# Ten pairs of gate and up blocks by seven products instead of nine, with the squares' sum and the gating moved into the first two pairs

## The chip, the core and the metric

The kernel runs on one core of a Trainium2 chip. A core has five engines with a queue each, worked off in order: TensorE (PE in the profile, its weight loads PEld), VectorE (DVE), ScalarE (ACT), GpSimd (POOL) and SyncE (SP), which here only issues DMAs. The metric is the device time of one execution in microseconds. The change is compared with the kernel before on the same chip.

## The reference

Two layers of an encoder trunk for 512 tokens of width 1024, all in float32: an attention, then a gated feed-forward block (2816 wide), both with a normalisation before and after. What the change touches is the feed-forward part and the last products of the attention ahead of it:

```python
def rms_norm(x, g):
    y = xf * lax.rsqrt(jnp.mean(xf * xf, axis=-1, keepdims=True) + EPS)
    return (y * g.astype(jnp.float32)).astype(x.dtype)

def swiglu(h, w_gate, w_up, w_down):
    return (jax.nn.silu(h @ w_gate) * (h @ w_up)) @ w_down

for layer in range(DEPTH):
    h = rms_norm(x, attn_pre_g[layer])
    ...
    x = x + rms_norm(y, attn_post_g[layer])
    h = rms_norm(x, ffn_pre_g[layer])
    f = swiglu(h, ffn_w_gate[layer], ffn_w_up[layer], ffn_w_down[layer])
    x = x + rms_norm(f, ffn_post_g[layer])
```

## The kernel before

**Tiles.** Activations lie feature by feature: a tile is [128 features, 512 tokens], x is eight of them. Every matmul operand is split into a high part (a cast to the fast float32 form, on ACT) and a low part (the difference, on DVE), and each product takes three matmuls: high by high, high by low, low by high (`mm3`, L375; `split`, L143). Weights come in pieces of [128, 1024]: `Feed` holds the order of all pieces (`plan`), loads them through a ring of five raw tiles on SP's queue and splits them one or two pieces ahead of their use, into rings of three high and three low tiles, or, where a piece is planned with room "h", into tiles of the feed-forward pool.

**Order.** The program is traced in Python, and a planner then puts each engine's queue in order: the instruction that is traced first goes first, if its operands and its tile are there in the planner's own reckoning. `first(n)` lets instructions count as traced n earlier, and `issue_after` (`behind`) sets one instruction behind another on the same queue, without a wait. A tile is taken from a ring with a tag when its first instruction is placed, and is free again when its last one is done. Tag "u" has 39 tiles of [128, 512] (L78, L87), tag "h" 40 (L1136). PSUM has eight banks: four with tag "mm", two with "s", two with "t" (L93).

**Stages of a layer.** Attention; `out_proj` (L683), whose last four output tiles are made in two token halves; `Post.add_half` (L631), which sums the squares of a half (`Sum.total`: transposes on TensorE into a bank "t", a sum on DVE), takes the power -1/2 on POOL (`rstd`, L478) and spreads the factor with transposes (`spread`, L494); `apply`, which adds the normalised result to x and splits the new x (xs, 16 tiles "u"). Then gate and up. Of 22 blocks of 128 features, 0 and 1 are done in token halves (L1147), so that TensorE can begin when half of x is there; 2 and 3 whole (L1184); the other 18 as nine pairs in `products` (L1514). The norm's factor (from the squares of x, L161 and L164, total and spread at L1173 to 1178) is not in xs; it multiplies the gate's output (L1193, L1561).

**A pair by seven products.** Two blocks of gate and the same of up, by two halves of the tokens (A0, A1) and two halves of the features, are a 2 by 2 block product; seven products of half-size operands replace eight. The token side's combinations (tb, 16 tiles "u") are built once a layer by `blocks_of` in three steps; the weight side's are made for each pair: a pair's pieces are loaded twice for two sums, the sums begun by DMAs that add (`Pair.begin`, on POOL's queue, behind the plain load) and continued by two DVE additions (`Pair.sums`, L183). For the first pair of a layer DVE makes the first two sums as well. A pair's products go to the banks `be` (products 0 and 6; two banks, "s" in even pairs, "t" in odd ones), `al` (1, 3, 4, 5) and `ga` (2). Results are copied or added out of the banks after each product into two gate and two up tiles (tag "u"). After product 6 the pair is gated: times the factor (DVE), Silu (ACT), times up (DVE, into `hd`), and for every second block four differences that the down projection needs (`Hidden.add`, L1251). The down projection (`down`) works by seven products too. In layer 1, steps of `by_tokens` (loads of x, DVE transposes, stores) are put between the pairs' products.

Of the kernel before, what the change touches and what calls it, by code (L numbers as in the profile page):

```python
# [19 lines left out]
KT = D // P  # L20
# [7 lines left out]
N_WHOLE = 4  # L28
# [40 lines left out]
def trunk(ctx: ExitStack, tc: tile.TileContext, a, out):  # L69
# [80 lines left out]

    class Pair:
# [4 lines left out]
        def __init__(self, src):  # L156
            self.src, self.raw, self.then, self.made = src, {}, None, False

        def tile(self, n, pool_=wp, tag="raw", bufs=5):
            t = pool_.tile([P, 1024], F32, tag=tag, name=name_("raw"), bufs=bufs)  # L160
            nc.sync.dma_start(t, self.src[n])  # L161
            return t

        def begin(self):  # L164

            r, self.made = self.raw, True
            r[0] = r[3] = r[6] = self.tile(2, wide[0], "sum", 2)
            r[4] = self.tile(2, wide[0], "sum2", 2)
            for j, n in ((0, 3), (4, 0)):
                nc.gpsimd.dma_start(r[j], self.src[n], accum_op=OP.add)  # L170

        def load(self, j):

            if j == 0:
                if not self.made:
                    self.raw[4] = self.tile(2, wide[0], "sum2", 2)
                self.raw[5] = self.tile(3)
            elif j in (1, 2):
                self.raw[j] = self.tile(j - 1)

        def sums(self, j):
# [81 lines left out]
    class Feed:  # L263


        def __init__(self):
            self.plan, self.raw, self.ready, self.pos, self.room = [], [], [], 0, {}
            self.behind, self.gate = {}, None
# [4 lines left out]
        def add_pairs(self, src):  # L273
# [3 lines left out]
            for p, pair in enumerate(pairs):  # L277
                pair.then = pairs[p + 1] if p + 1 < n else None
                for j in range(7):
# [8 lines left out]
        def load(self, i):  # L288
            while len(self.raw) <= min(i, len(self.plan) - 1):
# [5 lines left out]
                if isinstance(src, Pair):  # L295
                    src.load(j)
# [8 lines left out]
        def split(self, i):  # L305
            while len(self.ready) <= min(i, len(self.plan) - 1):
# [32 lines left out]
                for c in range(0, 0 if isinstance(raw, list) else n, w):  # L339
                    m = min(w, n - c)  # L340
                    with ExitStack() as st:
                        for b in self.behind.get(j, ()):
                            st.enter_context(tc.issue_after(b.ins))
                        if gain is None or isinstance(src, Pair):
                            split(pieces[c // w][0][:, :m], pieces[c // w][1][:, :m], raw[:, c:c + m])
                            continue
                        for d in range(0, m, S):
                            split_scaled(pieces[c // w][0][:, d:d + S], pieces[c // w][1][:, d:d + S],
                                         raw[:, c + d:c + d + S], gain[:, (c + d) // S, 0:1])
# [127 lines left out]

    def rstd(v):  # L478
        r = small("r")[:, :v.shape[1]]
        nc.gpsimd.tensor_tensor(r, v, mhalf[:, :v.shape[1]], op=OP.pow)  # L480
# [128 lines left out]
    class Post:  # L609
# [21 lines left out]
        def add_half(self, h, banks, rest, n1, n2, end=None):  # L631
# [3 lines left out]
            if end:  # L635
                feed.behind[feed.pos] = feed.behind[feed.pos + 1] = ins
# [4 lines left out]
            with first(200):  # L641
                r = rstd(v)
            at = some(rest, n2)
# [31 lines left out]
    def fetch(src, make=U):  # L675
        x = []
        for k in range(KT):
            t = make(name="x")
            nc.sync.dma_start(t, src[:, k])
            x.append(t)  # L680
        return x

    def out_proj(rhs, n_k, post, have, n_last, late):  # L683
# [35 lines left out]
        for h in range(2):  # L719
            k = KT - sum(last)  # L720
            for i, m in enumerate(last):
# [14 lines left out]
                k += m  # L736
        return b
# [110 lines left out]
    for k in range(KT):  # L848
# [17 lines left out]
        if k == 3:  # L866
# [261 lines left out]
    def ffn(i, x_src, osp, firsts, late=()):  # L1128
# [10 lines left out]
        x = fetch(x_src)  # L1139
        post = Post(G_APOST[i], H)  # L1140
        last = out_proj(osp, KT, post, firsts, 2, late)
# [25 lines left out]
        tb = []  # L1167
        more = blocks_of(x, G_FPRE[i], H, tb)
        next(more)
        b = [bank(), bank()]  # L1170
        rest = proj(2, KT, 4, xs, b)
        some(rest, 3)
        v = sx.sum.total()  # L1173
        r = rstd(v)
        eps = sp.tile([P, 4], F32, tag="eps", name=f"eps_{i}", bufs=1)
        V.tensor_scalar(eps, v, EPS, None, op0=OP.mult)
        some(rest, 7)
        rb = spread_sb(r)
        next(more)
        banks.extend(b)  # L1180
        hid = Hidden(H)


        for f in range(N_WHOLE):  # L1184
            if f < 3:
# [666 lines left out]
```

## Time and profile before

| | us |
|---|---|
| median of 3 runs | 1108.43 (1107.37 to 1109.54) |
| the profiled execution | 1108.42 |
| its span, first to last instruction | 1106.5 |
| layer 0: gate and up, blocks 2 and 3 | 213.3 to 236.0 |
| layer 0: nine pairs | 236.0 to 415.7 |
| layer 1: blocks 2 and 3 | 790.1 to 812.9 |
| layer 1: nine pairs | 812.9 to 993.1 |

Times in the views are microseconds from the span's start. A row of the timeline is start, length, engine, line, operation, output <- inputs, count, and in brackets how long the engine had been idle and what ended that. A row of groups is line, engine, operation, shapes, count, then busy time, mean length in ns, idle time before. A matmul is shown with a modelled end that overlaps the next one, so the pace of matmuls is read from a stretch and its count, not from a row's length. L145 is the low part and L144 the high part, whatever is split.

### The profile page before, as it was taken

To read this page: it belongs to the slowest core of one execution; us is meant where nothing else is said; L and a number is where in the kernel's file an instruction comes from. 1 tells how busy PE (TensorE), PEld (TensorE's weight loads), DVE (VectorE), ACT (ScalarE), POOL (GpSimd) and SP (SyncE) were. 2 spreads that over 40 slices of the span, in tenths; PEclk is the share of its full clock that TensorE was granted. 3 is DMA by queue.
4 is the path that set the end of the run, shared out by engine and by line. 5 is a ranking of instruction groups with operands and counts; after the bars stand their busy time and mean duration, and the time that the engine had idled before them with its cause. 6 is when DMAs were issued, how large, how long until landed. Compare 5 with 4: busy or idle time off the path is not lost. (4 is left out here: it accounts for less than half of the span.)

```text
span 1106.5 us, 19053 instructions
## 1 busy us (share of the span) xinstructions
PE 1092.9 (99%) x6893; PEld 978.6 (88%) x6893; DVE 908.8 (82%) x1651; ACT 679.0 (61%) x1319; POOL 118.2 (11%) x181
## 2 busy tenths in 40 slices
PE   9999999999999999999999999999999999999997
PEld 6887889999999998888888888889999999998885
DVE  7787747988878879978867888758988888889977
ACT  7575736755555556668635767656745555556675
POOL 2211100001000001500000110001000010002301
PEclk9999999999999999999999999999999999999999
DMA  7344227427677757961556677636438778859913
GB/s 239 117 118 138 66 69 256 153 76 193 171 205 182 178 171 247 160 193 47 190 146 169 166 193 189 162 115 215 162 92 214 207 198 220 210 177 280 172 29 76
DMA packets 88334, 181.47 MB, mean 164 GB/s; under 512 B 26816, under 2 KB 28608, under 8 KB 88240
## 3 DMA queue, kind: packets, MB, share of 16 engines
q1 hardware_dynamic: 74752, 147.10, 42.8%
q0 software_dynamic: 13056, 32.73, 16.7%
q8 instruction: 54, 0.88, 0.3%
q10 hardware_dynamic: 432, 0.44, 0.1%
q14 instruction: 40, 0.33, 0.1%
HBM read 148.88 MB, written 10.88 MB: 144 GB/s over the span
## 5 line engine op out<-in xcount | busy, mean ns | idle before, releaser
L144 ACT CAST whi<-raw 128x1024 fp32r<-128x1024 f32 (+3 forms) x224 | 225.4, 1006 | 218.2 <-PE al L1544 71.3
L145 DVE TENSOR_TENSOR wlo<-raw,whi 128x1024 fp32r<-128x1024 f32 (+3 forms) x224 | 261.0, 1165 | 62.9 <-ACT whi L144 61.9
L1544 PE MATMUL al<-th,whi 128*128 128x256 f32 x432 | 123.0, 285 | 0.2 <-ACT gt L1554 0.2
L1544 PE MATMUL al<-tl,whi 128*128 128x256 f32 x432 | 121.0, 280 | 0.0
L1544 PE MATMUL al<-th,wlo 128*128 128x256 f32 x432 | 121.0, 280 | 0.0
L376 PE MATMUL b<-xh,whi 128*128 128x512 f32 (+1 forms) x298 | 115.1, 386 | 0.0
L377 PE MATMUL b<-xl,whi 128*128 128x512 f32 (+1 forms) x298 | 109.9, 369 | 0.0
L378 PE MATMUL b<-xh,wlo 128*128 128x512 f32 (+1 forms) x298 | 109.5, 368 | 0.3 <-DVE wlo L145 0.3
L1544 PEld LDWEIGHTS al<-th,whi 128*128 128x128 f32 x432 | 81.3, 188 | 2.6 <-ACT gt L1554 0.4
L1544 PEld LDWEIGHTS al<-tl,whi 128*128 128x128 f32 x432 | 81.3, 188 | 0.0
L1544 PEld LDWEIGHTS al<-th,wlo 128*128 128x128 f32 x432 | 81.3, 188 | 0.0
L545 ACT ACTIVATE p<-p,mn 128x128 f32<-128x128 f32 (+1 forms) x96 | 54.1, 563 | 39.2 <-DVE mn L543 37.4
L145 DVE TENSOR_TENSOR ptl<-pt,pth 128x128 fp32r<-128x128 f32 (+1 forms) x96 | 46.6, 486 | 32.9 <-ACT pth L144 31.3
L145 DVE TENSOR_TENSOR wlo<-wd,whi 128x512 fp32r<-128x512 f32 x86 | 56.3, 685 | 14.6 <-ACT whi L144 14.4
L170 POOL DMA_DIRECT2D raw<-in_w_pair x32 | 28.0, 876 | 367.8 <-DMA raw<-in_w_pair 148.5
L378 PEld LDWEIGHTS b<-xh,wlo 128*128 128x128 f32 x298 | 56.2, 189 | 10.2 <-DVE wlo L145 0.7
L144 ACT CAST whi<-wd 128x512 fp32r<-128x512 f32 x86 | 49.8, 619 | 24.5 <-PE al L1300 10.7
L376 PEld LDWEIGHTS b<-xh,whi 128*128 128x128 f32 x298 | 56.5, 190 | 5.7 <-ACT whi L144 0.2
L377 PEld LDWEIGHTS b<-xl,whi 128*128 128x128 f32 x298 | 56.5, 190 | 5.5
L144 ACT CAST pth<-pt 128x128 fp32r<-128x128 f32 (+1 forms) x96 | 40.3, 422 | 30.3 <-PE pt L558 29.4
L1300 PE MATMUL al<-whi,pl 128*128 128x512 f32 x132 | 51.5, 390 | 0.0
L1300 PE MATMUL al<-whi,ph 128*128 128x512 f32 x132 | 51.4, 389 | 0.0
(319 smaller groups left out, 3301.0 us busy)
## 6 DMA issues: line engine op xcount, KB each, us to landing
raw<-in_w_pair SPq DMA_DIRECT2D x88, 512.0 KB, 4.4
raw<-in_w_pair POOLq DMA_DIRECT2D x32, 512.0 KB, 8.0
wd<-in_w_down SPq DMA_DIRECT2D x54, 256.0 KB, 6.0
raw<-in_w_o SPq DMA_DIRECT2D x16, 512.0 KB, 3.5
raw<-in_w_gu SPq DMA_DIRECT2D x16, 512.0 KB, 4.9
raw<-in_w_down SPq DMA_DIRECT2D x16, 512.0 KB, 4.2
raw<-in_w_qkb SPq DMA_DIRECT2D x16, 512.0 KB, 3.5
wd<-in_w_down POOLq DMA_DIRECT2D x22, 256.0 KB, 5.2
```

Source lines behind the costliest of these rows:

```text
L144: return (nc.scalar.copy(dst_hi, src), V.tensor_tensor(dst_lo, src, dst_hi.bitcast(F32), op=OP.subtract))
L145: V.tensor_tensor(dst_lo, src, dst_hi.bitcast(F32), op=OP.subtract))
L170: nc.gpsimd.dma_start(r[j], self.src[n], accum_op=OP.add)
L376: nc.tensor.matmul(o, l[0], r[0], start=start, stop=False)
L377: nc.tensor.matmul(o, l[0], r[1], start=False, stop=False)
L378: last_mm[0] = nc.tensor.matmul(o, l[1], r[0], start=False, stop=stop)
L545: nc.scalar.activation(p[:, :n], p[:, :n], AF.Exp, bias=mn[:, :1], scale=-1.0, accum_out=self.sums[:, qt:qt + 1])
L1300: nc.tensor.matmul(to[e], l[c], r[d], start=j < 4 and k == 0 and n == 0, stop=k == NF // 2 - 1 and n == 2, skip_group_check=True)
L1544: nc.tensor.matmul(o, l[c], r[d], start=first_ and n == 0, stop=k == K2 - 1 and n == 2, skip_group_check=True)
```

## The change

Blocks 2 and 3 become a tenth pair (`N_WHOLE` is 2). The first pair of a layer runs its products in the order 1, 2, 0, 3, 4, 5, 6, since products 1 and 2 need only x itself, and the three steps of `blocks_of` stand before its products 1, 2 and 0. The squares of x are summed before its products 3 and 5; the total and the factor (`norm`) are put before product 1 of the second pair, the factor's spread and the gating of blocks 0 and 1 (`gates`) before its product 2, and the gating of the first pair (`late`) before its product 4. Until then the banks of blocks 0 and 1 are copied to tiles "h" (`kept`), and the first pair's gate and up tiles are of tag "h" too.

Around this: all four pieces of w_gu0 get room "h"; the first pair's sums are begun by adding DMAs as well, begun inside `add_half`; adding DMAs are queued behind the last power on POOL; x is fetched behind the load of the first pair's second piece; in `add_half` the next six splits are held behind a copy of the factor (`fence`) instead of the next two behind the squares; a weight's gain in the second attention is queued behind the low part last traced; the positions are loaded three steps later at the start; `by_tokens` takes four steps a pair instead of three.

```diff
-N_WHOLE = 4
+N_WHOLE = 2
...
+    FIRST_TURN = (1, 2, 0, 3, 4, 5, 6)
...
             for j, n in ((0, 3), (4, 0)):
-                nc.gpsimd.dma_start(r[j], self.src[n], accum_op=OP.add)
+                with tc.issue_after(last_pow[0].ins):
+                    nc.gpsimd.dma_start(r[j], self.src[n], accum_op=OP.add)
...
-            if j == 0 and not self.made:
-                r[0] = r[3] = r[6] = wide[0].tile([P, 1024], F32, tag="sum", name=name_("raw"), bufs=2)
-                plus(r[0], r[4], r[5])
-            elif j in (3, 6):
+            if j in (3, 6):
                 plus(r[j], r[j], r[j // 3])
-            elif j == 4 and not self.made:
-                plus(r[4], r[4], r[1])
-            elif j == 1 and self.then:
+            if j == (3 if self.turn[0] else 1) and self.then:
                 self.then.begin()
...
-                        for b in self.behind.get(j, ()):
+                        for b in self.behind.get(j, ()) or (self.low,):
                             st.enter_context(tc.issue_after(b.ins))
                         V.tensor_tensor(rv, rv, gain, op=OP.mult)
...
-            if end:
-                feed.behind[feed.pos] = feed.behind[feed.pos + 1] = ins
             with behind(end):
                 at = some(rest, n1)
             with behind(end and at):
                 v = self.sum.total(h, 200)
             with first(200):
                 r = rstd(v)
+                fence = V.tensor_copy(small("f")[:, :v.shape[1]], r),
+            if not h:
+                with behind(feed.loaded):
+                    next(p for p, *_ in feed.plan[feed.pos:] if isinstance(p, Pair)).begin()
+            for n in range(len(feed.ready), len(feed.ready) + 6):
+                feed.behind[n] = fence
...
+            if not h:
+                feed.ahead(5)
+                feed.loaded = get_x(feed.loads[feed.pos + 5])
...
-            feed.add(a["w_gu0"][i, c], 1024, room="h" if c in (1, 2) else None)
-        for f in range(N_WHOLE - 2):
-            for c in range(2):
-                feed.add(a["w_gu"][i, f, c], 1024)
+            feed.add(a["w_gu0"][i, c], 1024, room="h")
...
-        if k == 3:
+        if k == 6:
             load_positions()
...
-        sx.squares(0)
         post.apply(x, 1, sx.each)
         run(half(1))
-        sx.squares(1)
...
+        kept = []
+        for b in banks:
+            kept.append(H(name="fu"))
+            nc.scalar.copy(kept[-1], b)
...
+        def norm():
+            v = sx.sum.total()
+            r = rstd(v)
+            V.tensor_scalar(eps, v, EPS, None, op0=OP.mult)
+            rb.append(r)
+
+        def gates():
+            rb[0] = spread_sb(rb[0])
+            for f in range(N_WHOLE):
+                t, u = kept[2 * f:2 * f + 2]
+                V.tensor_tensor(t, t, rb[0], op=OP.mult)
+                nc.scalar.activation(t, t, AF.Silu)
+                h = hid.room()
+                V.scalar_tensor_tensor(h, t, -1.0, u, op0=OP.mult, op1=OP.mult)
+                hid.add(h)
+
+        step = lambda: next(more)
+        side = {(0, 1): step, (0, 2): step, (0, 0): step, (0, 3): lambda: sx.squares(0), (0, 5): lambda: sx.squares(1),
+                (1, 1): norm, (1, 2): gates}
+        products(xs, tb, rb, hid, side, by_tokens(H) if i else None)
...
+            make = U if p else hid.make
+            gate = [make(name="gt") for _ in range(2)]
+            up_ = [make(name="ut") for _ in range(2)]
+            for j in (range(7) if p else FIRST_TURN):
+                if (p, j) in side:
+                    side[p, j]()
+                if (p, j) == (1, 4):
+                    late()
+                if aside is not None and p and j in (0, 1, 3, 5):
                     next(aside, None)
...
+                        if p:
+                            gated(t, u)
+
+            if not p:
+                late = lambda gate=gate, up_=up_: [gated(t, u) for t, u in zip(gate, up_)]
```

`gated(t, u)` is the factor, Silu, product and `hid.add` that stood in the loop before.

More of the change, by code (lines that the diff above doesn't have):

```diff
@@ L179, in load @@
                 self.raw[j] = self.tile(j - 1)
+                return self.last
         def sums(self, j):
@@ L267, in __init__ @@
             self.plan, self.raw, self.ready, self.pos, self.room = [], [], [], 0, {}
-            self.behind, self.gate = {}, None
+            self.behind, self.gate, self.low, self.loads = {}, None, None, {}
         def add(self, src, n, gain=None, room=None):
@@ L673, in apply, with fetch, out_proj @@
                     each(k, h)
[L675 to L683, printed above, removed]
+    def fetch(src, x, after=None):
+        with behind(after):
+            for k in range(KT):
+                t = U(name="x")
+                ins = nc.sync.dma_start(t, src[:, k])
+                x.append(t)
+        return ins
+    def out_proj(rhs, n_k, post, have, n_last, late, get_x):
         done = list(have)
```

82 lines of the change are left out of this document (26 added, 56 removed).

## The prediction

> **What bounds the kernel now.** I read the page's busy times first, then the clock row of its slices.
>
> ```profile
> PE 1092.9 (99%) x6893; PEld 978.6 (88%) x6893; DVE 908.8 (82%) x1651; ACT 679.0 (61%) x1319; POOL 118.2 (11%) x181
> PEclk9999999999999999999999999999999999999999
> ```
>
> TensorE is busy for 99% of the span at full clock. So time goes only where TensorE issues fewer columns, or where one of its waits goes; and any new wait of TensorE counts in full. Next, the view of waits for PE (in total us, times, longest):
>
> ```profile
> PE bc L498 <- POOL r L480: 1.9, 2, 1.4
> ...
> PE b L378 <- DVE wlo L145: 0.3, 1, 0.3
> PE al L1544 <- ACT gt L1554: 0.2, 1, 0.2
> ```
>
> The change can touch the first, the post-norm's factor (once a layer), and the second, at the start (w_aq's low part); the third is all that the pairs wait. Then busy time by stage (columns: stretch, length, PE, PEld, DVE, ACT, POOL, clock, DMA): blocks 2 and 3 and the nine pairs, of layer 0 and of layer 1, and block 3 of layer 0 alone.
>
> ```profile
> 213.25:235.98 22.73, 22.73 (x107) 18.81 (x105) 20.39 (x42) 15.15 (x25) 1.07 (x1) 1.00 0.21 70
> 235.98:415.66 179.68, 179.68 (x1514) 178.51 (x1512) 151.03 (x212) 99.53 (x157) 12.21 (x14) 1.00 0.67 180
> 790.10:812.88 22.78, 22.78 (x107) 18.86 (x106) 20.43 (x42) 15.15 (x25) 1.07 (x1) 1.00 0.22 70
> 812.88:993.09 180.21, 179.99 (x1514) 178.76 (x1512) 154.87 (x219) 99.54 (x157) 12.08 (x14) 1.00 0.74 198
> 225.10:235.98 10.88, 10.88 (x50) 9.01 (x48) 9.51 (x20) 4.32 (x7) 0.00 (x0) 1.00 0.04 16
> ```
>
> TensorE never rests there, and VectorE is close behind: 20.39 of 22.73 us in the blocks.
>
> **Fewer products.** Blocks 2 and 3 are 2 x 2 x 8 x 3 = 96 matmuls of 512 columns, and eight transposes (total and spread) that stay. A pair is 7 x 2 x 4 x 3 = 168 matmuls of 256 columns; it costs 179.68 / 9 = 19.96 us in layer 0 and 20.02 in layer 1. Block 3's row has its 48 in 10.88 us (the 50 count one more at each edge), 0.227 each, so two blocks are 21.8 us, and the other 0.9 of the 22.73 are the transposes. A layer saves 21.8 - 20.0 = 1.8 us, two save **3.7** (unrounded).
>
> The Trainium skill, "TensorE: Matmul & The Clock Gate", section "Back-to-back issue gap", speaks against such a change: it gives a sustained 131 ns for a matmul of 512 columns and 81 for one of 128, so half a width costs far more than half. By a line between these two (an estimate, 98 ns for 256) a layer would lose 3.9 us. The traces disagree: 227 ns against 119, nearly in proportion.
>
> **The post-norm's wait.** Token half 0 in both layers, rows in order of time (start, length, engine):
>
> ```profile
> 180.47 1.22 DVE L145 TENSOR_TENSOR wlo<-raw,whi 128x1024 fp32r<-128x1024 f32 x1 [2.18 <-ACT whi L144]
> 181.61 0.42 DVE L475 TENSOR_REDUCE ss<-tot 128x2 f32<-128x256 f32 x1
> 181.94 1.22 DVE L145 TENSOR_TENSOR wlo<-raw,whi 128x1024 fp32r<-128x1024 f32 x1
> 182.21 1.52 POOL L480 TENSOR_TENSOR r<-ss,mhalf 128x2 f32<-128x2 f32 x1 [12.96 <-DVE ss L475]
> 183.79 0.43 PE L498 MATMUL bc<-ident,r 128*128 128x128 f32 x2 [0.58 <-POOL r L480]
> 194.06 0.74 POOL L480 TENSOR_TENSOR r<-ss,mhalf 128x2 f32<-128x2 f32 x1 [10.33 <-DVE ss L475]
> 760.69 0.43 PE L498 MATMUL bc<-ident,r 128*128 128x128 f32 x2 [1.36 <-POOL r L480]
> ```
>
> A low part of 1.22 us stands ahead of the sum, the next runs beside POOL's power, which takes 1.52 us; in half 1, among small DVE operations, it takes 0.74. The change loads w_gu0 before x, splits it before this point, and holds the next six low parts behind a copy of r (the fence). Both waits should go: 0.58 + 1.36 = **1.9**. Bounds 0 (the splits of w_gu0 and of two pieces of the first pair are traced ahead of the fence) and 1.9; I take 1.9, since x's issues no longer stand ahead of w_gu0's, 168.6 - 163.3 = 5.3 us:
>
> ```profile
> 163.30 4.64 SPq L679 DMA_DIRECT2D x<-in_x  x8
> 168.56 14.96 SPq L302 DMA_DIRECT2D raw<-in_w_gu  x6
> x<-in_x SPq DMA_DIRECT2D x8, 256.0 KB, 6.7
> ```
>
> What is late next is x, whose issue now stands behind the first pair's second piece on SP's queue. It is first needed after the spread at 183.8 and lands 6.7 us after its issue, so it may be issued 13.8 us later than 163.3 at no cost. The six pieces then ahead of it took 15.0 us here, so the cost is 0 to 1.2 us a layer; I take 0, as the copy of the last of them waits for nothing but a slot that the earlier splits free.
>
> **The start.** The four position loads go behind w_aq's first piece on SP's queue, so this comes sooner and the wait of 0.3 for its low part goes, at most: **0.3**, bounds 0 and 0.3.
>
> **At nothing.** The first pair's two sums go from DVE to adding DMAs on POOL's queue (which has 11% work; the new order behind the power keeps a power from waiting behind them). The gain's place behind the last low part in attention 1, and four instead of three steps of the token transposes a pair, move DVE work where TensorE waits for nothing in the list. The four copies of the banks cost ACT 4 x 0.6 us, which has 9 us free in a pair; the first pair starts with products 1 and 2, which need no new operand, and its third bank pair first 5.7 us in.
>
> **VectorE.** Here the change adds. Groups of DVE rows in blocks 2 and 3, then in one pair (busy us, mean ns), and windows around them:
>
> ```profile
> L145 DVE TENSOR_TENSOR wlo<-raw,whi 128x1024 fp32r<-128x1024 f32 x4 | 4.9, 1222 | 0.5 <-ACT whi L144 0.5
> L1193 DVE TENSOR_TENSOR gt<-b,bc 128x512 f32<-128x512 f32 x2 | 1.3, 682 | 0.0
> L475 DVE TENSOR_REDUCE ss<-tot 128x4 f32<-128x512 f32 x1 | 0.7, 682 | 0.0
> ...
> L145 DVE TENSOR_TENSOR wlo<-raw,whi 128x1024 fp32r<-128x1024 f32 x7 | 8.6, 1223 | 2.7 <-ACT whi L144 2.7
> L183 DVE TENSOR_TENSOR raw<-raw,raw 128x1024 f32<-128x1024 f32 x2 | 2.4, 1222 | 0.0
> L1564 DVE TENSOR_TENSOR hd<-gt,ut 128x512 f32<-128x512 f32 x2 | 1.3, 687 | 0.0
> L1552 DVE TENSOR_TENSOR gt<-gt,ga 128x256 f32<-128x256 f32 x2 | 0.7, 416 | 0.0
> L1265 DVE TENSOR_TENSOR hs<-hd 128x256 f32<-128x256 f32 x1 | 0.4, 421 | 0.0
> ```
> ```profile
> 189.80:201.60 11.80, 11.80 (x101) 11.80 (x100) 11.60 (x29) 8.55 (x23) 1.61 (x2) 1.00 0.58 165
> 201.60:213.25 11.65, 11.65 (x99) 11.65 (x98) 11.65 (x33) 7.16 (x16) 0.00 (x0) 1.00 0.44 165
> 235.98:255.90 19.92, 19.92 (x170) 19.79 (x169) 17.48 (x25) 10.98 (x17) 0.91 (x1) 1.00 0.54 157
> 255.90:275.90 20.00, 20.00 (x171) 19.87 (x170) 16.78 (x24) 10.95 (x18) 2.61 (x3) 1.00 0.72 185
> ```
>
> Gone: four low parts 4.9, gating of two blocks 2.6, the first pair's two sums 2.4 = 9.9 us. New: seven low parts 8.6, two sums 2.4, six additions of banks (three couples like L1552's) 2.3, gating of two 2.6 = 15.9. From 189.8 to the end of the next pair DVE had 11.6 + 11.65 + 20.39 + 17.48 = 61.1 us of work in 66.1. It gets 67.1 in 64.3, and must push some 3 us and its pauses into later pairs, which have 20.00 - 16.78 = 3.2 free each. That would do if gating, which nobody on TensorE awaits, were what is late.
>
> **The new wait.** It isn't free to be late. The total of x's squares and the spread of its factor are put at products 1 and 2 of the second pair. Both need a bank of tag "t", of which there are two, and the second pair's own `be` (odd pairs take "t") holds both from its product 0 to the addition after its product 6. So they can stand on TensorE's queue only at that pair's end (call it E), and the gating of blocks 0 and 1, of the first pair and of the second all starts after it. The factor takes four transposes, a sum of 0.68, a power of 1.07, four transposes and a copy of 0.57, some 3.2 us. These rows give the durations, and the first two what follows a gating:
>
> ```profile
> 261.31 0.42 DVE L1266 SCALAR_TENSOR_TENSOR hs<-hs,hd 128x256 f32<-128x256 f32 x1
> 261.64 0.42 DVE L1267 TENSOR_TENSOR hs<-hd,hd 128x256 f32<-128x256 f32 x1
> 218.34 1.07 POOL L480 TENSOR_TENSOR r<-ss,mhalf 128x4 f32<-128x4 f32 x1 [22.66 <-DVE ss L475]
> 221.65 0.57 ACT L505 COPY bc<-bc 128x512 f32<-128x512 f32 x1
> 260.31 0.37 ACT L1550 COPY gt<-al 128x256 f32<-128x256 f32 x1 [0.15 <-PE al L1544]
> ```
>
> Begun 0.8 before E (the first `be` has its last product 1.4 before E, then its addition), it is there at E + 2.4. Now the tiles: of 39 of tag "u", xs holds 16, tb 16, the second pair 4, the factor 1, and the third pair's two up tiles the rest. Its gate tiles wait until the second pair is gated. Ahead of this on DVE stand two blocks (2.6 us, four differences 1.3, as they start 0.33 apart), the first pair (2.6 and 1.3), then two factors and one product of the second pair (2.0): 9.8 us, so E + 12.2, and the copy of product 1 lands at E + 12.6. TensorE needs it for product 3, at 3 x 2.85 + 0.7 = E + 9.3. The row at 260.31 shows the same copy before: TensorE was late, not the tile. Price per layer: at least 0 (if the second pair were gated first: E + 4.8), 3.3 by this order, 4.4 with product 3's own low part behind the gating, 7.5 with two low parts, a sum and two additions between. I take 4.4, nearest to the order of the code: **8.8** for two layers.
>
> **Sum.** Made against the profiled run, 1108.42 us (span 1106.5 and 1.92 around it; the median of the runs is 1108.43): 1108.4 - 3.7 - 1.9 - 0.3 + 8.8 = **1111.3 us**.
>
> **Rivals.** (1) Faster, the other side: the gating's wait doesn't come, because the queues are drawn up so that the total and the spread stand ahead of the second pair's `be`, or the second pair is gated early. Then 1111.3 - 8.8 = 1102.5. For it: before, TensorE has no wait over 0.2 us in 360 us of pairs, and DVE has 3.2 us free in each. It decides where the third pair's first copy lands before E + 9.3. Chance 0.35; and 0.07 more for the same with the post-norm's waits kept, 1104.4. (2) VectorE is late already in the first pair (40 operations of 0.33 us for squares and new operands and four of 0.6, beside seven low parts 8.6, two sums 2.4 and additions 2.3: 29 us, from the end of x's second half, some 6 us ahead of the pair, to its end: 26), each layer 1 to 2 us more and the gating at its 7.5: 1120. Chance 0.05. (3) Half-width matmuls cost three quarters of whole ones: at 0.170 us instead of 0.119 a pair would be 28.6 us and each layer lose 6.8, 1108.4 + 13.6 - 2.2 = 1120; the 18 pairs at 20.0 us in the rows exclude it but for 0.01. The Trainium skill's section named above would have it so.
>
> **How the numbers follow.** The forecast's case has 0.52: its price runs from 3.7 to 15 for two layers, 1106 to 1117.5 us. Runs of this kernel tell 0.2%, 2.2 us, from no change: same is 1106.2 to 1110.6, a third of this case (0.17); slower is the rest, 0.35, with rivals 2 and 3: 0.41. Faster is rival 1 in both forms, 0.42. The range that leaves out 2 in 10 goes from 1101 to 1115; the likeliest case alone is 1107 to 1116.
>
> **What would show it.** Blocks and pairs: 19.96 us a pair and 168 more matmuls a layer less 96. Waits: bc <- POOL gone, or x named in its place. The new wait: PE al L1544 waiting for the copy of product 1 in the third pair, and the transposes of the total standing after the second pair's last product. I am wrong if these stand inside the second pair, or if no wait over 1 us shows in the third.

## The result and the profile after

| | before | after |
|---|---|---|
| median of 4 runs, us | 1108.99 (1107.37 to 1112.59) | 1142.95 (1142.69 to 1143.94) |
| profiled execution, us | 1108.42 | 1143.94 |
| its span, us | 1106.5 | 1142.2 |

The ratio is 1.0282, with a 95% interval of 1.0253 to 1.0312: slower by 34 us. Ratios are of fast runs alone; one execution of a later experiment (the total in the first pair), at 2169.57 us, is left out of them. The direction was the forecast's, by luck as much as by judgement, since its chances were 0.41 for slower and 0.42 for faster; the size was not, and the time lies far outside the range. The page of after, its busy times and its clock row:

```profile
PE 1105.0 (97%) x7037; PEld 993.2 (87%) x7037; DVE 920.2 (81%) x1677; ACT 693.7 (61%) x1353; POOL 123.4 (11%) x189
PEclk9999999998999999999999999999999999999999
```

TensorE has 144 matmuls more, as forecast (2 x (168 - 96)). Its idle time grew from 1106.5 - 1092.9 = 13.6 to 37.2 us, and its busy time by 12 us although there is less to multiply. Matmuls last longer where the clock is lower, and the mean granted clock is 0.989 instead of 0.998; besides, a matmul beside a wait counts as busy for more than its place in the pace (in the first row by stage below, 24.74 us at clock 1.00 for 199 matmuls that take 23.45 without waits), so idle time alone understates what a wait costs. The view of waits for PE (in total us, times, longest):

```profile
PE al L1555 <- DVE wlo L145: 6.8, 6, 2.1
PE al L1555 <- ACT gt L1561: 5.3, 2, 2.7
PE b L375 <- ACT xh L148: 3.1, 2, 2.0
PE bc L499 <- POOL r L481: 2.9, 4, 0.9
PE al L1555 <- ACT whi L144: 2.3, 2, 1.2
...
PE b L376 <- DVE xl L149: 1.9, 3, 0.9
```

The list now names operands of x (xh, xl), low parts of weights and the copies into gate tiles. The view of windows by stage shows where they stand (columns as before): for each layer blocks 0 and 1, then the first, second and third pair, then the other seven.

```profile
188.77:215.73 26.96, 24.74 (x199) 23.76 (x197) 16.69 (x43) 9.18 (x20) 4.29 (x5) 1.00 0.85 249
215.73:242.95 27.22, 22.52 (x170) 21.49 (x169) 24.38 (x51) 23.76 (x53) 0.87 (x1) 0.94 0.34 90
242.95:262.95 20.00, 20.00 (x169) 19.76 (x167) 15.36 (x20) 9.94 (x15) 0.86 (x1) 1.00 0.60 169
262.95:292.07 29.12, 24.38 (x179) 23.78 (x178) 24.62 (x42) 14.73 (x23) 3.69 (x4) 0.88 0.61 143
292.07:431.94 139.87, 139.87 (x1170) 139.03 (x1169) 115.98 (x163) 77.77 (x123) 9.60 (x11) 1.00 0.69 180
...
783.58:811.96 28.38, 25.47 (x198) 25.07 (x197) 16.69 (x43) 9.17 (x20) 4.29 (x5) 0.94 0.81 236
811.96:839.45 27.49, 23.16 (x170) 21.88 (x169) 24.30 (x53) 23.83 (x53) 0.85 (x1) 0.94 0.32 90
839.45:859.46 20.01, 20.01 (x169) 19.77 (x167) 15.86 (x20) 9.88 (x15) 0.86 (x1) 1.00 0.67 194
859.46:887.40 27.94, 23.19 (x178) 22.59 (x178) 25.25 (x42) 14.75 (x23) 3.67 (x4) 0.94 0.57 122
887.40:1028.13 140.73, 140.73 (x1179) 139.89 (x1178) 119.94 (x172) 77.92 (x123) 9.46 (x11) 1.00 0.78 213
```

The loss has three places in each layer, and nothing of it is in the second or in the last seven pairs. Blocks 0 and 1 took 23.45 and 23.39 us before: +3.5 and +5.0. The first pair takes 27.2 and 27.5 instead of 19.96 and 20.02: +7.3 and +7.5. The third takes 29.1 and 27.9; without the 0.9 for the total's and the factor's transposes that is +8.2 and +7.0. Together 38.5; the pair in place of two blocks gives back 3.7 (22.73 less 0.9 less 20.0, twice), and the rest of the span is 0.9 us longer.

What ends the idle time at the three places, in the timeline. Blocks 0 and 1 (ACT, POOL, PE):

```profile
191.29 0.51 ACT L148 ACTIVATE xh<-x,gains 128x256 fp32r<-128x256 f32 x1 [0.49 <-DVE x L675]
197.54 1.05 ACT L144 CAST whi<-raw 128x1024 fp32r<-128x1024 f32 x1 [5.73 <-DMA raw<-in_w_pair]
198.50 0.51 ACT L148 ACTIVATE xh<-x,gains 128x256 fp32r<-128x256 f32 x1
189.42 0.97 POOL L173 DMA_DIRECT2D raw<-in_w_pair  x1 [5.40 <-ACT y L619]
199.05 0.38 PE L375 MATMUL b<-xh,wh 128*128 128x256 f32 x1 [1.06 <-ACT xh L148]
```

ScalarE stands for 5.73 us at the cast of a weight sum whose adding DMA was issued at 189.42 and landed 8.1 us later. Behind it in the queue is the operand xh that TensorE needs. First pair (DVE, ACT, PE):

```profile
217.55 0.43 DVE L1318 TENSOR_TENSOR t<-xg 128x256 f32<-128x256 f32 x1 [6.57 <-ACT xg L1317]
214.85 2.06 ACT L1173 COPY fu<-b 128x512 f32<-128x512 f32 x4 [4.38 <-PE b L377]
216.76 1.37 ACT L1317 ACTIVATE xg<-x,gains 128x512 f32<-128x512 f32 x2
231.95 0.39 PE L1555 MATMUL al<-th,wlo 128*128 128x256 f32 x1 [2.10 <-DVE wlo L145]
```

The four copies of the banks wait for the blocks' last matmul, and the first scaled x for the new operands (xg) stands behind them; VectorE rests for 6.57 us and then has 24.4 us of work in the pair, and TensorE's longest wait there is for a low part of a weight. End of the second and third pair (PE):

```profile
262.95 0.66 PE L471 MATMUL tot<-ident,acc 128*128 128x128 f32 x4
265.51 0.65 PE L499 MATMUL bc<-ident,r 128*128 128x128 f32 x4 [0.84 <-POOL r L481]
276.35 0.38 PE L1555 MATMUL al<-th,whi 128*128 128x256 f32 x1 [2.68 <-ACT gt L1561]
278.35 0.58 PE L1555 MATMUL al<-th,wlo 128*128 128x256 f32 x1 [1.23 <-DVE wlo L145]
```

The total stands at 262.95, the end E of the second pair, and product 3 of the third waits for the copy until E + 13.4, as drawn in the prediction (E + 12.6, then the low part). Behind that wait the clock falls:

```profile
277.75:284.25 6.50, 5.90 (x27) 5.90 (x28) 5.62 (x9) 1.53 (x3) 0.00 (x0) 0.50 0.39 113
```

27 matmuls in 6.5 us, half the usual pace. By the trace's clock record, after has five such stretches, four of 3.4 us and one of 6.8, 20.5 us together, which cost at most half of that, 10.2 us (a part of them lies in waits). Before had one of 3.4 us (at 108 us, behind a wait of 1.92 us). Both have a last one at the very end, when TensorE is done.

### The profile page after: what moved, and what is told of

It is laid out like the page before. It is cut to its first block, busy times and chain, and to the rows that moved or that the text cites. A ratio compares the mean times of both kernels' runs of the same rounds, so it can differ in the third digit from the quotient of the medians.

```text
span 1142.2 us, 19462 instructions
## 1 busy us (share of the span) xinstructions
PE 1105.0 (97%) x7037; PEld 993.2 (87%) x7037; DVE 920.2 (81%) x1677; ACT 693.7 (61%) x1353; POOL 123.4 (11%) x189
## 4 chain that ended last, share of the span: by engine, by line
PE 80%; DVE 6%; DMA 5%; issue 4%; ACT 3%; POOL 1%; SPq 0%; DVEq 0%; POOLq 0%; ACTq 0%
PE al L1555 16%; PE b L375 8%; PE b L376 8%; PE b L377 8%; PE al L1298 8%; PE be L1555 7%; PE be L1298 5%; PE ga L1555 3%; DMA raw<-in_w_pair 3%; PE de L1298 3%; PE ga L1298 3%; PE pt L559 2%; PE b L1712 2%; DVE wlo L145 1%; PE b L1106 1%
## 5 line engine op out<-in xcount | busy, mean ns | idle before, releaser
L144 ACT CAST whi<-raw 128x1024 fp32r<-128x1024 f32 (+4 forms) x226 | 227.3, 1007 | 209.4 <-PE al L1555 72.1
L145 DVE TENSOR_TENSOR wlo<-raw,whi 128x1024 fp32r<-128x1024 f32 (+4 forms) x226 | 263.7, 1168 | 77.9 <-ACT whi L144 76.4
L1555 PE MATMUL al<-th,whi 128*128 128x256 f32 x480 | 140.1, 292 | 8.4 <-ACT gt L1561 5.3
L1555 PE MATMUL al<-th,wlo 128*128 128x256 f32 x480 | 138.2, 290 | 6.8 <-DVE wlo L145 6.8
L375 PE MATMUL b<-xh,whi 128*128 128x512 f32 x170 | 71.8, 423 | 0.0
L145 DVE TENSOR_TENSOR ptl<-pt,pth 128x128 fp32r<-128x128 f32 (+1 forms) x96 | 46.8, 487 | 30.0 <-ACT pth L144 29.1
L377 PE MATMUL b<-xh,wlo 128*128 128x512 f32 x170 | 67.0, 394 | 0.3 <-DVE wlo L145 0.3
L376 PE MATMUL b<-xl,whi 128*128 128x512 f32 x170 | 66.8, 393 | 0.0
L144 ACT CAST whi<-wd 128x512 fp32r<-128x512 f32 x86 | 49.9, 619 | 24.9 <-PE al L1298 10.7
L1298 PE MATMUL al<-wlo,ph 128*128 128x512 f32 x132 | 51.4, 389 | 0.0
L185 DVE TENSOR_TENSOR raw<-raw,raw 128x1024 f32<-128x1024 f32 x40 | 49.0, 1225 | 0.6
L1555 PE MATMUL be<-xh,wlo 128*128 128x256 f32 x160 | 45.0, 283 | 1.2 <-DVE wlo L145 1.2
```

The source lines that it names most:

```text
L144: return (nc.scalar.copy(dst_hi, src), V.tensor_tensor(dst_lo, src, dst_hi.bitcast(F32), op=OP.subtract))
L145: V.tensor_tensor(dst_lo, src, dst_hi.bitcast(F32), op=OP.subtract))
L185: V.tensor_tensor(t, x, y, op=OP.add)
L375: nc.tensor.matmul(o, l[0], r[0], start=start, stop=False)
L376: nc.tensor.matmul(o, l[0], r[1], start=False, stop=False)
L377: last_mm[0] = nc.tensor.matmul(o, l[1], r[0], start=False, stop=stop)
```

## The experiments

Each ratio is to the kernel before, with its 95% interval. The kernel before was run again beside each group of experiments, and its median lay between 1108.99 and 1110.37 us; differences of 2 us between runs of two groups are therefore not clear of noise. Single runs have no interval.

**Three single edits and their sum.** The first exchanges the banks of `be`:

```diff
-            be = [bank("t" if p % 2 else "s", "be") for _ in range(2)]
+            be = [bank("s" if p % 2 else "t", "be") for _ in range(2)]
```

> The changed kernel with the banks of be exchanged: even pairs take tag t, odd pairs tag s. Theory (the total of x's squares waits for a bank of tag t that the second pair's be holds): the four transposes of the total stand at products 1 and 2 of the second pair, the third pair loses its waits (0.84 for the power, 2.68 for the copy of product 1, 1.23 for the low part behind the gating) and the 1.7 to 3.4 us at half clock that follow them; its stage falls from 29.1 and 27.9 us to about 20, the transposes move to the second pair (20.9), the total falls by some 15 us, from 1143 to 1128. Rival (VectorE is behind anyway after the first pair, or the tiles of tag u run out whatever the bank): the transposes move, but the third pair keeps a wait of 2 us or more and the total stays above 1138.

1133.73 us, ratio 1.0214 (1.0197 to 1.0230): 9.2 us less than after. The timeline has the total in the second pair, and the windows (second and third pair of layer 0) show where the wait went:

```profile
246.33 0.60 PE L471 MATMUL tot<-ident,acc 128*128 128x128 f32 x4
```
```profile
243.48:268.97 25.49, 23.63 (x182) 23.02 (x181) 22.30 (x38) 13.73 (x21) 4.58 (x4) 0.93 0.65 150
268.97:288.41 19.44, 19.44 (x167) 19.31 (x165) 17.19 (x25) 10.78 (x17) 0.99 (x2) 1.00 0.71 177
```

The bank was the cause of the wait in the third pair: it is gone in both layers. But the second pair now takes 25.5 and 25.0 us and waits for high and low parts of weights, with VectorE, which now gates two blocks and a pair there, busy for 22.3 of the 25.5 us. Both theories had a part.

The second writes the first step of new operands ahead of the copies:

```diff
+        next(more)
         kept = []
         for b in banks:
             kept.append(H(name="fu"))
             nc.scalar.copy(kept[-1], b)
...
-        side.pop((0, 1))()
```

> The changed kernel with the first of the three steps of new operands written ahead of the four copies of the banks. Theory (ScalarE's queue: the copies wait for the last product of the blocks, and the operands stand behind them, so that VectorE rests 6.6 us ahead of the first pair): VectorE's idle stretch before its first operand falls below 2 us, the first pair from 27.2 and 27.5 us to 21 to 23, the total falls by 8 to 13 us, to 1130 to 1135. Rival (the first pair's work on VectorE and ScalarE, some 24 of its 27 us, is too much wherever it starts): the first pair stays above 25 us and the total above 1139.

1136.01 us, ratio 1.0238 (1.0221 to 1.0254): 6.9 less. VectorE's first operand stands at 211.81, inside the blocks, and the first pair takes 24.5 and 24.9 us instead of 27.2 and 27.5. The place in ScalarE's queue is worth some 2.7 us a layer; 4.5 of the 7.3 stay, so the theory expected too much of it.

The third holds the split of product 0's sum behind the last operand of x (`end` is the last split that `each` made):

```diff
         post.apply(x, 1, sx.each)
+        feed.behind[len(feed.ready)] = sx.end
         run(half(1))
```

> The changed kernel with the split of product 0's weight sum held behind the last operand of x's second half. Theory (ScalarE's cast of the sum, which waits 5.7 us for the adding DMA, stands ahead of the operands of x's first half): the stage of blocks 0 and 1 falls from 27.0 and 28.4 us to about 23.4, PE no longer waits for xh and xl, the total falls by some 8.5 us to 1134.5. Rival (x itself lands too late, since its fetch was moved behind the pair's second piece): the waits for xh stay, now put down to x's DMA, and the total stays above 1140.

1134.27 us, ratio 1.0218 (1.0200 to 1.0237): 8.7 less, as the theory had it. Blocks 0 and 1 have no wait left in either layer, with x fetched where the change fetches it:

```profile
190.62:214.07 23.45, 23.45 (x199) 23.45 (x197) 16.92 (x43) 9.12 (x20) 4.28 (x5) 1.00 0.96 283
```

> All three edits together. If the three losses are independent (8.5 in the blocks, 14.8 in the first pairs of which 10 to 13 go, 15.3 in the third pairs), 1143 falls to 1104 to 1109. If they are one backlog of VectorE that is only passed on, the sum falls short of the single gains by 5 us or more and the total is over 1115.

1122.20 us, ratio 1.0113 (1.0098 to 1.0128): 20.8 less; the single gains sum to 24.8. The total is over 1115, as the theory of one backlog has it, though the sum falls short by 4.0 and not by 5: most of the gains add up, and a part of the wait is passed on. The blocks are whole, the third pairs too; first pairs 24.6, second pairs 26.0 and 26.7 us.

**VectorE's work.** The squares back at their old places, alone and with the three edits:

```diff
+        sx.squares(0)
         post.apply(x, 1, sx.each)
         run(half(1))
+        sx.squares(1)
...
-        side = {(0, 1): step, (0, 2): step, (0, 0): step, (0, 3): lambda: sx.squares(0), (0, 5): lambda: sx.squares(1),
+        side = {(0, 1): step, (0, 2): step, (0, 0): step, 
```

> The changed kernel with the squares of x back at their old places (half 0 after the post-norm of half 0, half 1 after the blocks' last matmul), nothing else. Theory (the first pair holds more VectorE work, 24.4 us in 27.2, than the pair is long, and it starts only when ScalarE's copies are done): the 16 squares and sums take 5.3 us of VectorE out of the pair, the first pair falls from 27.2 and 27.5 us to 22 to 25, the total by 4 to 10 us from 1143. Rival (only the place in ScalarE's queue counts, the squares come late in the pair and delay nothing): the first pair stays within 1 us, the total above 1140.

1139.34 us, ratio 1.0260 (1.0224 to 1.0295): 3.6 less, which the intervals alone don't tell from no gain. First pairs 25.4 and 25.9 us, gains of 1.9 and 1.6: between the two theories.

> Banks exchanged, first operands ahead of the copies, product 0's split behind x's operands, and the squares back at their old places. Theory (what is left of the loss after the three edits, 4.6 us in each first pair and 5 to 6 in each second, is VectorE's work that doesn't fit the first pair): first pair 20 to 22 us, second 21 to 24 (its transposes 0.9 among it), PE's waits there under 2 us a layer, the clock whole; total 1106 to 1112 from 1122. Rival (the second pair's gating of five factors at once is what is late, whenever it starts): second pair stays at 25 to 26.5 us, total 1113 to 1118.

1118.85 us, ratio 1.0070 (1.0051 to 1.0089). First pairs 24.1 and 24.3, second 26.5 and 24.0: the rival was nearer. The windows of the first pair of layer 0, without and with this edit, show why the first pair barely shrank:

```profile
211.67:236.26 24.59, 20.71 (x171) 20.07 (x170) 21.04 (x43) 20.61 (x46) 0.87 (x1) 1.00 0.41 105
```
```profile
212.80:236.91 24.11, 21.05 (x170) 20.02 (x169) 21.10 (x39) 17.04 (x33) 0.87 (x1) 1.00 0.39 110
```

VectorE is as busy in it as before: ten operations for squares left the pair (4.3 us), and two more weight additions and four more operations for new operands (4.1 us) took their place.

Other places for the factor and the gating. All in the first pair, which then gates itself at its end:

```diff
-                (1, 1): norm, (1, 2): gates}
+                (0, 4): norm, (0, 6): gates}
```

> First operands ahead of the copies, product 0's split behind x's operands, squares back, and the total and the gating of blocks 0 and 1 put into the first pair (total at product 4, factor at product 6; banks of be as in the changed kernel), so that the first pair is gated at its own end like the others. Theory: if the late factor is what made the second or third pair long, every pair from the second on takes 20 us and the first 21 to 23 (transposes 0.9 among it); total 1101 to 1106, below the kernel before (1108.4 less 3.7 for the products, 1104.7). Rival (VectorE's work of the first pair, operands 13 us and ten weight operations 12 us and gating 2.6, exceeds the pair): the first pair is 24 us or more and PE waits there for a low part; total 1109 to 1114.

1116.30 us, ratio 1.0056 (1.0037 to 1.0074). First pairs 25.8 and 25.9 with the transposes, of which 1.75 is the wait for the power; second 21.2 and 21.4. The rival's case, though the total is 2 us over its range.

The gating over two pairs (`spread_r` is the spread alone):

```diff
+                (1, 1): norm, (1, 2): spread_r, (1, 5): gates}
...
-            make = U if p else hid.make
+            make = U if p > 1 else hid.make
...
+                if p == 2 and j in (1, 4):
+                    late[j // 4]()
```

> The kernel with all four edits (banks, operands, product 0's split, squares), and besides the gating of blocks 0 and 1 moved from product 2 to product 5 of the second pair, that of the first and of the second pair into the third pair (products 1 and 4; the second pair's sums kept in tiles of tag h). Theory (VectorE's backlog: each pair has some 3 us of VectorE free, and what the second pair cannot hold may be done in the third): second pair from 26.5 and 24.0 us to 21 to 22.5 (transposes 0.9 among it), third 20 to 21, total 1110 to 1114 from 1119. Rival (the work is only passed on: the third pair grows by what the second loses): total 1117 or more.

1114.54 us, ratio 1.0037 (1.0021 to 1.0052), the theory's case, if slightly over its range: second pairs 22.6 and 21.9, third 19.7 and 20.0. Work that the second pair couldn't hold cost nothing in the third.

The factor in the first pair, the gating in the second:

```diff
+                (0, 3): norm, (0, 6): spread_r, (1, 1): gates}
```

> As the kernel with total and gating in the first pair, but only the total (product 3) and the factor (product 6) there, and the gating of blocks 0 and 1 and of the first pair in the second pair (products 1 and 4). Theory (the first pair has more VectorE work than its 20 us hold): first pair from 25.8 to 23 to 24.5 us, second 20 to 21.5, total 1110 to 1114 from 1116. Rival (PE's wait for the power, 1.75 us, and the operands set the first pair whatever is gated): first pair stays at 25 us or more, total 1115 to 1118.

1114.21 us, ratio 1.0038 (1.0022 to 1.0054): first pairs 24.9 and 25.5, second 20.7 and 21.3. The second pairs and the total are the theory's, or nearly, but the first pairs lie above its 24.5, and the one of layer 1 (with clock 0.93) is in the rival's range. The gain of 2.1 us over the run before the last is not clear of noise. Both of these kernels are some 0.4% slower than the kernel before.

**GpSimd in VectorE's stead.** The sums of squares on GpSimd (`on`), in both of these kernels:

```diff
-                    ins += V.tensor_tensor(t, t, q[:, c], op=OP.add),
+                    ins += self.on.tensor_tensor(t, t, q[:, c], op=OP.add),
```

> The kernel with the gating spread over the second and third pair, and besides the additions of x's squares to their sum (12 operations of 128x256 a layer, 0.33 us each on VectorE, 4 us) given to GpSimd. Theory (VectorE's work is what is left of the loss: 80.9 us busy of 89.8 from the blocks to the third pair's end): the first pair falls from 24.1 to 20.5 to 22.5 us, the total from 1114.5 to 1108 to 1112. Rival (the operands of the first pair come one behind another, from ScalarE to VectorE and back, and set it whatever else VectorE has to do): the first pair stays above 23.5 us, the total at 1113 to 1116.

> The same edit on the kernel with total and factor in the first pair and the gating in the second. Theory: first pair from 24.9 and 25.5 to 21.5 to 23.5 us, second 20 to 21.3, total 1106 to 1111 from 1114. Rival (the total now waits for GpSimd's additions, slower than VectorE's, and the factor comes later than product 6): first pair 25 us or more, total 1114 or more.

1122.08 us, ratio 1.0113 (1.0094 to 1.0132), and 1120.45, ratio 1.0094 (1.0076 to 1.0112): 7.5 and 6.2 us more instead of less. In the first run the first pairs take 26.8 and 27.5 us and the total lies outside both ranges. The second has the rival's figures, with first pairs of 28.0 and 28.1 us, but not its cause: TensorE waits for the total 0.5 us in all. The groups of DVE rows from the blocks to the second pair, in the kernel with the spread gating and then with the sums on GpSimd (the POOL row is of the whole run, both layers):

```profile
L149 DVE SCALAR_TENSOR_TENSOR xl<-x,gains,xh 128x256 fp32r<-128x256 f32 x13 | 6.0, 479 | 0.0
L675 DVE TENSOR_TENSOR x<-x,y 128x256 f32<-128x256 f32 x13 | 5.2, 418 | 0.0
```
```profile
L149 DVE SCALAR_TENSOR_TENSOR xl<-x,gains,xh 128x256 fp32r<-128x256 f32 x13 | 7.6, 600 | 0.2 <-ACT xh L148 0.2
L676 DVE TENSOR_TENSOR x<-x,y 128x256 f32<-128x256 f32 x12 | 7.2, 623 | 0.0
...
L462 POOL TENSOR_TENSOR acc<-acc,sq 128x256 f32<-128x256 f32 x24 | 21.3, 887 | 14.0 <-DVE acc L458 12.0 <-ACT xh L148 0.7
```

VectorE's operations beside GpSimd's grew from 418 to 623 and from 479 to 600 ns; the low part of a new operand (128x256) took 0.96 us at 213.35, while GpSimd was adding, and 0.41 at 216.78, when it was done. The operands came late, and so did the copies of the banks behind them on ScalarE, for which product 2 of the first pair now waits:

```profile
217.56 0.41 ACT L144 CAST th<-t 128x256 fp32r<-128x256 f32 x1 [1.32 <-DVE t L1326]
217.88 0.58 ACT L1181 COPY fu<-b 128x512 f32<-128x512 f32 x1
218.51 0.39 PE L1562 MATMUL ga<-xh,whi 128*128 128x256 f32 x1 [1.43 <-ACT fu L1181]
```

Blocks 0 and 1 took 24.7 us instead of 23.45.

**What the first pair still holds.** The kernel with the spread gating, less VectorE's two weight additions in the first pair, so that products 3 and 6 there take unfinished sums:

```diff
-            if j in (3, 6):
+            if j in (3, 6) and not self.turn[0]:
```

> The kernel with the gating spread over the second and third pair (1114.5 us), but without VectorE's two additions of weights in the first pair of each layer (products 3 and 6 take the unfinished sum): 2 x 1.22 us of VectorE's work left out of the first pair, everything else the same. Theory (the first pair's 24.1 us are VectorE's 21.1 us of work and its pauses): the first pair falls by 1.5 to 3 us, to 21 to 22.6. Rival (the chain of a product's operands, cast on ScalarE, low part on VectorE, sets it; VectorE has slack): it falls by less than 0.8 us.

1112.42 us, a single run. The first pairs, with the spread gating and then less the additions:

```profile
213.15:237.26 24.11, 21.05 (x171) 20.03 (x169) 21.10 (x39) 17.02 (x33) 0.87 (x1) 1.00 0.37 102
...
793.50:817.67 24.17, 21.04 (x170) 20.02 (x169) 21.16 (x39) 17.09 (x33) 0.85 (x1) 1.00 0.40 119
```
```profile
213.19:236.72 23.53, 22.30 (x170) 21.50 (x169) 18.61 (x36) 16.80 (x33) 1.00 (x2) 0.93 0.33 89
791.67:814.26 22.59, 21.12 (x170) 20.08 (x169) 18.58 (x36) 16.86 (x33) 0.85 (x1) 1.00 0.28 76
```

Layer 1 gains 1.6 us for 2.5 us of work, the theory's case. Layer 0 gains 0.6, but its clock is 0.93 there, a loss of 0.07 x 23.5 = 1.6 that the pair compared with hasn't. That a clock of 1.00 would have given layer 0 the same gain is argued, not shown. Nor does the edit tell VectorE's load from the chain of operands: an addition is also a link of that chain, ahead of ScalarE's cast and the low part. So the additions are worth some 1.6 us of the first pair; by which way, and what the 2.6 us are that stay in layer 1, is open.

**Waits and the clock.** The kernel before, with repeated copies on ScalarE that make product 3 wait:

```diff
                     elif j == 1:
+                        for _ in range({2: 16, 4: 19, 6: 22, 8: 25}.get(p, 0) * (1 - e)):
+                            nc.scalar.copy(t[:, A0], o)
                         nc.scalar.copy(t[:, A0], o)
```

> The kernel before, in which ScalarE copies product 1 of one half 17, 20, 23 and 26 times in the third, fifth, seventh and ninth pair instead of once, so that TensorE waits for the last copy ahead of product 3, some 0.5 to 4 us by the copy's 0.3 us. Theory (a wait costs itself and, from some length on, a stretch at half clock): after waits that sum to about 1.7 us or more the clock stands at 0.50 for 3.4 us (1.7 us lost) or twice that; after shorter ones it stays at 1.00. Rival (the half clock belongs to something else in the changed kernel, such as VectorE's or the DMAs' load): no low clock after any of the eight waits.

1146.40 us, a single run. No low clock after any wait, the longest included, as the rival has it; windows over that wait and behind it:

```profile
419.39:422.18 2.79, 0.03 (x1) 0.00 (x0) 0.02 (x1) 2.58 (x8) 0.00 (x0) 1.00 0.63 222
422.18:432.00 9.82, 8.80 (x65) 8.28 (x66) 5.49 (x8) 4.70 (x6) 0.00 (x0) 1.00 0.45 151
```

So a wait of 2.8 us may pass without low clock (the last section shows why). With 28 to 37 extra copies instead:

> The kernel before with 29, 32, 35 and 38 copies on ScalarE instead of 17 to 26, so that TensorE waits longer ahead of product 3 in the third, fifth, seventh and ninth pair, some 3 to 7 us. Theory (the clock falls when more than about half of some fixed 3.4 us lies idle, so a wait of 1.6 to 3 us may or may not hit, and one of over 3.4 us always does): low clock for 3.4 us or twice that after each wait of over 3.4 us. Rival (waits in the middle of the pairs don't lower the clock, whatever their length): no low clock after any.

1212.50 us, a single run. All eight waits, of 3.4 to 7.6 us, were followed by low clock, so the rival falls; the first of them:

```profile
290.85:294.28 3.43, 0.00 (x1) 0.01 (x1) 0.02 (x1) 3.16 (x9) 0.73 (x1) 1.00 0.56 84
295.75:302.25 6.50, 5.58 (x26) 5.28 (x26) 2.44 (x3) 2.36 (x3) 0.19 (x1) 0.50 0.24 81
```

The low stretches are 6.8 us long for the waits of 3.4 us, 10.2 for those of 4.6 and 5.8, 13.7 for those of 7.6. The longer ones begin while TensorE still waits, where there is nothing to slow down; behind the wait remain 6.8 to 9.6 us, so each wait loses 3.4 to 4.8 us besides itself.

## Why the prediction was wrong, and where right

- **Fewer products: right.** The seven later pairs take 139.87 / 7 = 19.98 and 20.10 us. Half-width matmuls keep 0.119 us in after too. The gaps of 131 and 81 ns of the Trainium skill, "TensorE: Matmul & The Clock Gate", section "Back-to-back issue gap", would have made them dearer; the trace doesn't bear that out. The 3.7 us were gained.
- **The new wait of the gating: right in place and nearly in size, wrong as a price.** The total stands at the second pair's end and product 3 of the third waits; 4.4 a layer was forecast, the waits are 0.84 + 2.68 + 1.23 = 4.75 and 4.74. The 0.84 for the power wasn't in the sum. The clock was not either: it cost some 3.0 us in layer 0 (6.8 us at half clock, of which 0.8 lie in the wait) and 1.7 in layer 1. The step "any new wait of TensorE counts in full" failed on the low side: it counts in full and can halve the clock behind it. Rival 1 was wrong in its price: with the total early (the exchanged banks) the third pair is whole, but the second is 5 us longer.
- **"At nothing": the step that failed most.** "The first pair's two sums go from DVE to adding DMAs on POOL's queue" was priced by POOL's load and not by who waits for the sum: ScalarE's cast of it, in order, ahead of x's operands. It cost 3.5 and 5.0 us (up to 1.7 of the latter by low clock), shown by the edit that moves this cast alone. "The four copies of the banks cost ACT 4 x 0.6 us, which has 9 us free" counted their time and not their place: they hold the operands behind them, about 2.7 us a layer, shown by the edit that writes the operands first.
- **Rival 2, VectorE late in the first pair: right in kind, at a chance of 0.05 and 1 to 2 us.** It measured 7.3 and 7.5. Its 29 us of work were set against a start "some 6 us ahead of the pair"; the start was 1.8 us into it (217.55). Of the 7.3, up to 1.7 is the clock. The prediction's sum, 67.1 us of work in 64.3 (its six additions of banks are 2.1 us by the row, not 2.3), let the surplus fall on the gating, for which TensorE doesn't wait; in the trace TensorE waited in the first pair for low parts of weights, up to 2.10 us at once. The edits account for 2.7 (the copies' place) and 1.6 to 1.9 (the squares, alone); the rest of the first pair's loss stays open.
- **The post-norm's wait, -1.9: wrong.** The power no longer runs beside a low part (0.73 us instead of 1.52), but PE's waits are 0.59 and 0.60: the plan now leaves 7 matmuls between total and spread, where 21 stood before. In layer 1 the gain of 0.76 is taken back by new waits ahead of the total (0.55 for the sum, 0.23 for y). The start's 0.3 stayed as well (0.26).
- **x behind the pair's second piece at 0: right**, by the whole blocks of that same edit.

Forecast and profiled run differ by 1143.9 - 1111.3 = 32.6 us: blocks 0 and 1 8.5, first pairs 14.8, third pairs 15.2 - 8.8 = 6.4, the post-norm and the start some 2, down and the later pairs about 1.

## What to carry to other kernels

An operation that moves to an idle queue is not free: ask which queue consumes its result, what stands behind the consumer there, and when the result can land. Price an operation on ScalarE or VectorE by its place, since four copies of half a microsecond that wait for a matmul hold everything behind them. And where TensorE never rests, as here, a stage in which VectorE is busy for 20.39 of 22.73 us had little room for more, and GpSimd was no place for it: its additions made VectorE's slower.

## What the runs showed of the hardware

**The clock falls on a fixed grid of 3.41 us, after less than a whole idle window.** In all sixteen profiles low clock is 0.50. By the trace's clock record its stretches begin whole multiples of 3.413 us apart within a profile and last one such length or several (the one at the very end is cut off). In after they begin at 233.22, 277.59, 796.42, 823.73 and 874.93 us, which is 13, 152, 8 and 15 lengths apart. Each profile was cut into windows on its own grid, from the first clock record to 16 us before the end, and TensorE's idle time taken in each. Of 5030 windows at full clock with under 1.2 us idle none was followed by a low one; of 66 with 1.2 to 1.78 us 15 were; of 34 with more, 33. (Idle time is blurred by modelled ends and missing records.) A low window was followed by another in all 21 cases with 0.6 us idle or more, and by a full one in all 48 with less than 0.45.

So it matters how a wait lies on the grid. The wait of 1.92 us in the first attention falls into one window in the kernel before, and the next is low; in after two windows share it, with 1.57 and 0.36 us idle, and neither is followed by a low one:

```profile
104.61:108.02 3.41, 1.49 (x9) 0.98 (x7) 2.94 (x5) 3.36 (x6) 0.91 (x2) 1.00 0.57 153
108.02:111.44 3.42, 3.42 (x15) 3.29 (x14) 2.80 (x8) 1.19 (x5) 0.90 (x2) 0.50 0.97 304
```
```profile
103.51:106.93 3.42, 1.85 (x12) 1.31 (x10) 2.21 (x5) 3.33 (x7) 0.75 (x1) 1.00 0.51 113
106.93:110.34 3.41, 3.05 (x18) 2.61 (x19) 3.41 (x10) 1.89 (x6) 1.06 (x2) 1.00 0.90 308
```

The 2.8 us that passed without low clock were shared likewise, as windows with 1.61 and 1.71 us idle. The Trainium skill, "TensorE: Matmul & The Clock Gate", section "Part 1: The HAM clock gate (the "warmup" mystery)", has a free-running window of 3.4 us after which an idle array goes to half clock; the length and the grid agree. Its idle time of a whole window doesn't: about 1.8 us, some half of one, sufficed.

**GpSimd's additions slow VectorE's operations by a quarter to a half** in their mean (479 to 600, 418 to 623 ns). The Trainium skill, "SBUF — State Buffer", section "Who interferes with whom", says that the two share a pair of ports; these rows agree with that.
